# Attention steps put into a written-out cycle and pinned to program order on four engines

## Chip, core and metric

One core of a Trainium2 chip runs the whole kernel as one launch. The metric is the time of one launch in microseconds (us) of device time, lower is better; the time before is the median of three runs. All durations below are from one profiled execution of the kernel before.

## What is computed

One layer of a trunk: modulated RMS norm, one input projection, three token mixers (chunked gMLP, grouped-query attention, short gated convolution), an output projection, and a gated ConvFFN. The change lies in the attention, 1024 queries against 256 context keys and 1024 latent keys, 8 query heads in 2 key/value groups of 64 wide heads, in float32:

```python
def latent_attention(q, k_lat, v_lat, k_ctx, v_ctx):
    keys = jnp.concatenate([k_ctx, k_lat], axis=1)
    vals = jnp.concatenate([v_ctx, v_lat], axis=1)
    ...
    def block(qi):
        s = jnp.einsum('bqgrd,bkgd->bgrqk', qi, keys, preferred_element_type=jnp.float32) * ATT_SCALE
        p = jax.nn.softmax(s, axis=-1).astype(vals.dtype)
        return jnp.einsum('bgrqk,bkgd->bqgrd', p, vals)
    o = lax.map(block, qb)
```

## The kernel before

The attention is 16 units: 8 blocks of 128 queries times 2 key/value groups; a unit holds four heads. float32 products are made of a rounded part and a rest (fp32r), so each matmul below comes twice. Tiles and engines of one unit:

- `sc` (PSUM, one buffer): scores of two heads against the 256 context keys; four matmuls each on TensorE (PE).
- `sl` (PSUM, two buffers): scores of one head against the 1024 latent keys, four matmuls in two halves.
- VectorE (DVE) takes the row maxima of `sc` and `sl` and their common one (a 128x1 operation); ScalarE (ACT) writes the exponentials into `pp` (latent) and `pc` (context) with their row sums; DVE adds the two sums and takes the reciprocal (two 128x1 operations); GpSimd (POOL) multiplies `pc` and `pp` by it in place.
- `tr` (PSUM, two buffers): ten steps, one for each 128 keys, in which PE transposes the four heads' probabilities. ACT copies `tr` rounded into `ph`, DVE writes the rest `pw = tr - ph` (four buffers each), and PE adds value x `ph` and value x `pw` to `acc` (PSUM, one buffer).
- Tail: ACT copies the lower half of `acc` to `sh`, DVE adds the two halves into `af` (two operations), POOL splits `af` into two parts of `att`.

Helpers record every operation, so all rows of the profile show line 90. In the code, `scores` (line 281) makes the steps of the score part and `av` (line 973) those of the rest. Line 41 holds a cycle of tokens that is walked once for each unit (line 1015): `c` `a` `b` `p` `e` `z` are score steps of the newest unit, and `T`, `A`, `F` with a suffix are steps of a unit one or two cycles older. Three of these tokens stand for steps of several engines: `c` is matmul and maximum, `e` both exponentials, `z` sums, reciprocal and both POOL multiplications; `T` is transposes, copy and rest.

```python
PROG = "c0 T8+2 A5+2 a0 T9+2 b0 A6+2 A7+2 p0 e0 T0+1 A8+2 A9+2 F0+2 a1 T1+1 ..."
```

The tokens only say in what order the steps are recorded. From line 740 on nothing is pinned (`order("")`), so a scheduler in the compiler sets the order of each engine's queue from its own costs. Once built, each engine works through its queue strictly in that order; an instruction that waits holds up all behind it.

Into the cycle four kinds of side work are recorded at fixed points (`EV`, cycle number and fraction): `make_gB0` at 10.3 (PE makes two tiles `pgb` in the `tr` tag, ACT copies them to `gB`), `make_acm` at 11.3 (ACT rounds and DVE subtracts four `aT` and `cmT` slices of 128x512, two and two in one operation), and `w_out_part` four times at 11.5, 13, 15 and 15.1: it loads a piece `wo` of the output weights, POOL multiplies it by `gB` (two operations), ACT rounds it, DVE subtracts (`wos`). The first unit's scores are made earlier, between the matmuls `pcb` of the convolution gate (`X0`, line 40). Behind the attention the output projection (`po`) reads `acm`, `att` and `wos`.

Of the kernel before, what the change touches and what calls it, by code (L numbers as in the profile page):

```python
# [39 lines left out]
X0 = ("c0 a0 b0 p0 e0 z0 a1 b1 p1 e1 z1", "c1 a2 b2 p2 e2 z2 a3 b3 p3 e3 z3", "")  # L40
PROG = "c0 T8+2 A5+2 a0 T9+2 b0 A6+2 A7+2 p0 e0 T0+1 A8+2 A9+2 F0+2 a1 T1+1 b1 p1 e1 T2+1 c1 T3+1 z0 A0+1 a2 b2 p2 a3 A1+1 z1 e2 T4+1 T5+1 A2+1 A3+1 z2 b3 T6+1 p3 e3 A4+1 z3 T7+1"
AVO = sorted((i + 1000 * int(t[3:]), int(t[1])) for i, t in enumerate(PROG.split()) if t[0] == "A")
AVF, AVL = AVO[0][1], AVO[-1][1]
# [28 lines left out]
def trunk(  # L72
# [207 lines left out]

    def scores(tb, g):
        hf, i = tb // 4, tb % 4
        pl = []
# [30 lines left out]

        def soft(h):
            if h == 0:
# [5 lines left out]
                pl.append(box["pc"])  # L322
            if h % 2 == 0:
                box["pp"] = hp.tile([P, 2, NT], F32, name=f"pp{tb}{g}{h}", tag="h0", bufs=4)
            p_ = box["pp"][:, h % 2, :]
            pl.append(p_)
            S.activation(p_, box.pop(("sl", h)), AF.Exp, bias=v(2, h), accum_out=v(3, h))
            S.activation(box["pc"][:, h, :], box["sc"][:, h % 2, :], AF.Exp, bias=v(2, h),
                         accum_out=v(4, h))
# [7 lines left out]
        ops = {"c": ctx_mm, "a": lambda h: lat_mm(h, 0), "b": lambda h: lat_mm(h, 1),  # L337
               "p": top, "e": soft, "z": norm}

        def item(t):  # L340
            for o in t.split():
                ops[o[0]](int(o[1]))

        return item, pl
# [608 lines left out]
    def w_out_part(i):
        n2, q = i // 4, i % 4
        r = raw(f"wo{i}").rearrange("p (k n) -> p k n", k=2)
        dma(r, w_out[q * 256:(q + 1) * 256, n2 * 512:(n2 + 1) * 512]
            .rearrange("(k p) n -> p k n", p=P))
# [4 lines left out]
        wos.append(t_)

    with t_ctx:
# [7 lines left out]

        def av(tb, g, pl):
            hf, i = tb // 4, tb % 4
            box = {}
# [12 lines left out]
            def av_step(kb):
                if kb == AVF:
                    box["acc"] = pst.tile([P, 512], F32, name=f"acc{tb}{g}", tag="acc", bufs=1)  # L990
                acc = box["acc"]
# [2 lines left out]
                T.matmul(acc, vv, ph, start=kb == AVF, stop=False)
                T.matmul(acc, vv, pw, start=False, stop=kb == AVL)

            def fin(_):
                acc = box["acc"]
                sh = tp.tile([64, 512], F32, name=f"sh{tb}{g}", tag="sh", bufs=1)
                S.copy(sh, acc[64:128, :])  # L1000
                af = tp.tile([P, 2, P], F32, name=f"af{tb}{g}", tag="af", bufs=1)
                a4 = acc[0:64, :].rearrange("p (i e t) -> p i e t", i=2, e=2)
                s4 = sh.rearrange("p (i e t) -> p i e t", i=2, e=2)
# [4 lines left out]
                G.tensor_scalar(hi, af, 1.0, 1.0, ALU.mult, ALU.mult)
                G.tensor_tensor(lo, af, f(hi), ALU.subtract)

            return tr_step, av_step, fin

        xs, vs = {}, {0: av(0, 0, pl0)}
        prog = PROG.split()
        for n in range(len(prog), 20 * len(prog)):
            u_, at = n // len(prog), n % len(prog)
            if at == 0 and u_ < 16:
                xs[u_], pl = scores(u_ // 2, u_ % 2)
                vs[u_] = av(u_ // 2, u_ % 2, pl)
            t = prog[at]  # L1020
            if t[0] in "TAF":
                k, d = t[1:].split("+")
                if 0 <= u_ - int(d) < 16:
                    vs[u_ - int(d)]["TAF".index(t[0])](int(k))
            elif u_ < 16:
                xs[u_](t)
# [576 lines left out]
```

## Time and profile before

| | |
|---|---|
| time, median of 3 runs | 1302.74 us (1302.57 to 1303.81) |
| the profiled execution | 1302.53 us, of which the span from first to last instruction is 1300.7 us |
| busy share of the span | PE 95%, DVE 75%, ACT 47%, POOL 36% |
| attention, first score matmul to last `acc` matmul | 249.7 to 519.4 us |
| tail copies `sh<-acc`, one for each unit | first at 284.18 us, last at 519.38 us |

The attention takes about a fifth of the span. The copy `sh<-acc` comes once in each unit, so the distance of two of these copies is the period of the cycle. A row of the time line gives start, duration, engine, operation, output and input tiles (buffer numbers left out), and in brackets the engine's idle time before it and what ended it. Two instructions of one engine overlap a little at their ends, so the cost of one in a full queue is the distance from its start to the next start, not its duration.

### The profile page before, as it was taken

The numbers are of one execution on the slowest core, as the hardware profiler recorded it, in microseconds if no ns is written. First come the engines' busy times: TensorE is split into PE (matmuls) and PEld (weight loads), VectorE is DVE, ScalarE is ACT, GpSimd is POOL, SyncE is SP. The second block draws the span as 40 slices with busy tenths as digits, with TensorE's granted clock in tenths as the row PEclk, the third lists the DMA queues.
The fourth block names the chain that finished last, engine by engine and source line by source line (L and its number), as shares of the span: only waits on it lengthen the run. The fifth ranks groups of instructions, "written<-read, shape, count | busy, mean of one in ns | idle before, by whom it ended". The sixth has DMA issues, their size and how long they took to land.

```text
span 1300.7 us, 17813 instructions
## 1 busy us (share of the span) xinstructions
PE 1242.1 (95%) x6420; PEld 1028.0 (79%) x6420; DVE 978.5 (75%) x1700; ACT 614.2 (47%) x1116; POOL 463.0 (36%) x445
## 2 busy tenths in 40 slices
PE   6989999999998899999799999999999999999997
PEld 3879899877776677888588888888888888878885
DVE  4797777389989997686989899998678765225545
ACT  5753234277777777124554344344444534213331
POOL 1252243044446543542655544544453110030001
PEclk9999999999999999999899999999999999999999
DMA  9906001000000000963033433332230349023741
GB/s 289 280 19 193 28 31 50 17 1 2 1 2 1 1 1 19 326 195 142 0 98 98 130 97 103 124 98 90 89 98 33 130 173 363 15 95 132 259 178 65
DMA packets 109190, 132.15 MB, mean 102 GB/s; under 512 B 7632, under 2 KB 77998, under 8 KB 109102
## 3 DMA queue, kind: packets, MB, share of 16 engines
q1 hardware_dynamic: 109102, 131.01, 30.2%
q8 instruction: 51, 0.84, 0.3%
q14 instruction: 37, 0.30, 0.1%
HBM read 111.07 MB, written 19.92 MB: 101 GB/s over the span
## 4 chain that ended last, share of the span: by engine, by line
PE 83%; DVE 7%; ACT 4%; issue 2%; POOL 2%; DMA 1%; SPq 0%; POOLq 0%; DVEq 0%; ACTq 0%
PE pd L90 19%; PE pY L90 14%; PE pZ L90 9%; PE pX L90 9%; PE acc L90 5%; PE po L90 5%; PE tr L90 4%; PE pq L90 3%; PE sl L90 3%; PE pau L90 2%; PE pcc L90 2%; PE pcb L90 2%; PE pav L90 2%; PE pch L90 2%; PE sc L90 1%
## 5 line engine op out<-in xcount | busy, mean ns | idle before, releaser
L90 PE MATMUL pd<-wd,gt 128*128 128x512 f32 x912 | 209.2, 391 | 3.2 <-DVE wd L90 3.2
L90 PEld LDWEIGHTS pd<-wd,gt 128*128 128x128 f32 x912 | 172.1, 189 | 39.8 <-DVE wd L90 3.9
L90 PE MATMUL pY<-HT,wM 128*128 128x512 f32 x792 | 192.9, 392 | 6.7 <-DVE HT L90 3.9
L90 PEld LDWEIGHTS pY<-HT,wM 128*128 128x128 f32 x792 | 148.8, 189 | 39.4 <-DVE HT L90 4.4
L90 DVE TENSOR_TENSOR wM<-wu,wM 128x512 fp32r<-128x512 f32 x132 | 135.0, 1025 | 12.7 <-ACT wM L90 12.3
L90 ACT CAST wM<-wu 128x512 fp32r<-128x512 f32 x132 | 80.6, 620 | 111.3 <-PE pY L90 54.9
L90 PE MATMUL pX<-HB,wM 128*128 128x512 f32 x528 | 127.4, 389 | 0.0
L90 DVE TENSOR_TENSOR pw<-tr,ph 128x512 fp32r<-128x512 f32 x160 | 108.9, 684 | 14.2 <-ACT ph L90 13.6
L90 ACT CAST ph<-tr 128x512 fp32r<-128x512 f32 x160 | 92.1, 596 | 56.0 <-PE tr L90 55.3
L90 PEld LDWEIGHTS pX<-HB,wM 128*128 128x128 f32 x528 | 99.0, 188 | 20.5
L90 PE MATMUL sl<-K,Q 128*128 128x512 f32 x256 | 82.8, 408 | 8.1 <-ACT pp L90 8.1
L90 POOL TENSOR_TENSOR wu<-S,wu 128x512 f32<-128x512 f32 x22 | 29.4, 1335 | 169.9 <-DVE wM L90 169.7
L90 POOL TENSOR_SCALAR pc<-pc,sm 128x256 f32<-128x256 f32 x64 | 31.8, 497 | 148.5 <-DVE sm L90 102.7
L90 PE MATMUL tr<-ident,pp 128*128 128x128 f32 x512 | 80.1, 275 | 4.3 <-DVE pw L90 4.3
L90 PEld LDWEIGHTS tr<-ident,pp 128*128 128x128 f32 x512 | 61.7, 140 | 25.1 <-DVE pw L90 12.0
L90 DVE TENSOR_REDUCE sm<-sl 128x1 f32<-128x1024 f32 x64 | 77.5, 1213 | 0.4
L90 ACT CAST gt<-g 128x512 fp32r<-128x512 f32 x38 | 23.5, 619 | 108.3 <-DMA g<-gud 79.2
L90 ACT ACTIVATE pp<-sl,sm 128x1024 f32<-128x1024 f32 x64 | 72.2, 1128 | 4.8 <-DVE sm L90 4.7
L90 POOL TENSOR_SCALAR pp<-pp,sm 128x1024 f32<-128x1024 f32 x64 | 73.0, 1141 | 0.0
L90 DVE TENSOR_TENSOR wd<-wd,wd 128x1024 fp32r<-128x1024 f32 x44 | 55.7, 1266 | 18.0 <-ACT wd L90 15.7
L90 DVE TENSOR_TENSOR gt<-g,gt 128x512 fp32r<-128x512 f32 x38 | 26.1, 687 | 56.1 <-ACT gt L90 56.1
L90 PE MATMUL pZ<-HT,wM 128*128 128x512 f32 x264 | 66.1, 396 | 1.6 <-DVE HT L90 1.6
(341 smaller groups left out, 2798.1 us busy)
## 6 DMA issues: line engine op xcount, KB each, us to landing
wu<-in_ffn_up SPq DMA_DIRECT2D x88, 256.0 KB, 3.1
wd<-in_ffn_down SPq DMA_DIRECT2D x44, 512.0 KB, 7.8
w<-in_w_mod SPq DMA_DIRECT2D x24, 512.0 KB, 4.4
g<-gud SPq DMA_DIRECT2D x44, 256.0 KB, 4.7
wm<-in_w_mod SPq DMA_DIRECT2D x16, 512.0 KB, 6.7
wi<-in_w_in SPq DMA_DIRECT2D x16, 512.0 KB, 6.1
gud<-y SPq DMA_DIRECT2D x11, 512.0 KB
gud<-ya SPq DMA_DIRECT2D x11, 512.0 KB, 2.9
```

The lines of the kernel that those rows point to most:

```text
L90: i = fn(*a, **k)
```

## The change

`scores` and `av` no longer give compound tokens but one token for each step of one engine, and line 41's cycle is written anew over 83 tokens with suffix `+1` or `+2` for steps of the unit one or two cycles older. The letters, used from here on: on PE `C` context scores, `a` and `b` latent scores, `T` transposes, `A` the two products with the values; on DVE `x` and `p` maxima, `m` common maximum, `n` sum and reciprocal, `L` rest, `d` sum of the halves; on ACT `c` and `e` exponentials, `K` rounded copy, `f` tail copy; on POOL `y` and `z` multiplications, `g` output. `order("TVSG")` pins PE, DVE, ACT and POOL to the recorded order through the whole cycle. The `wo` loads are recorded one cycle before the other work on them (`WOL`), and the last two pieces move from 15 and 15.1 to 16.1 and 16.3. The accumulation now always goes from key block 0 to 9.

```diff
-WO0 = (11.5, 13, 15, 15.1)
-PROG = "c0 T8+2 A5+2 a0 T9+2 b0 A6+2 A7+2 p0 e0 T0+1 A8+2 A9+2 F0+2 ... z3 T7+1"
+WO0 = (11.5, 13, 16.1, 16.3)
+WOL = 1
+X0 = ("C0 x0 a0 b0 p0 m0 e0 c0 n0 y0 z0 a1 b1 ...", "C1 x1 a2 b2 ...", "")
+PROG = ("a0 L5+2 m3+1 n1+1 L6+2 z1+1 A4+2 b0 y1+1 T7+2 c3+1 K7+2 e3+1 p0 A5+2 C0 T8+2 A6+2 "
+        "K8+2 L7+2 T9+2 n2+1 x0 n3+1 m0 L8+2 K9+2 y2+1 a1 c0 y3+1 A7+2 b1 e0 L9+2 z3+1 z2+1 "
+        "A8+2 T0+1 K0+1 A9+2 f+2 T1+1 K1+1 p1 m1 a2 b2 L0+1 T2+1 d+2 A0+1 c1 L1+1 C1 T3+1 e1 "
+        "g+2 a3 K2+1 p2 K3+1 A1+1 L2+1 T4+1 K4+1 b3 A2+1 x1 L3+1 m2 T5+1 e2 n0 K5+1 L4+1 A3+1 "
+        "T6+1 z0 K6+1 y0 p3 c2")
...
-        def norm(h):
+        def recip(h):
             V.tensor_scalar(v(5, h), v(3, h), v(4, h), None, ALU.add)
             V.reciprocal(v(6, h), v(5, h))
-            for t_ in (box["pc"][:, h, :], pl[h + 1]):
-                G.tensor_scalar(t_, t_, v(6, h), 1.0, ALU.mult, ALU.mult)
+        def norm(h, at):
+            G.tensor_scalar(pl[at, h], pl[at, h], v(6, h), 1.0, ALU.mult, ALU.mult)
...
-        EV += [(w, lambda: w_out_part(len(wos))) for w in WO0]
+        EV += [(w - WOL, lambda i=i: w_out_part(i)) for i, w in enumerate(WO0)]
+        EV += [(w, lambda i=i: w_out_split(i)) for i, w in enumerate(WO0)]
...
+            def hi_step(kb):
+                ph = box["ph", kb] = tp.tile([P, 512], F32R, name=f"ph{tb}{g}{kb}", tag="ph",
+                                             bufs=PH)
+                S.copy(ph, box["tr", kb])
+            def lo_step(kb):
+                pw = box["pw", kb] = tp.tile([P, 512], F32R, name=f"pw{tb}{g}{kb}", tag="pw",
+                                             bufs=PH)
+                sub_lo(pw, box.pop(("tr", kb)), box["ph", kb])
...
+        order("TVSG")
+        for n in range(len(prog), (16 + lags) * len(prog)):
...
+            o, k, l = prog[at]
+            if 0 <= u_ - l < 16 and not (u_ == l and o in ops0):
+                us[u_ - l][o](k)
             for e, f_ in EV:
                 if n == int(e * len(prog)):
                     f_()
+        order("")
```

No instruction is added or removed on any engine, and the queue of SP, which issues all loads and stores, keeps its order. Three places follow; `sm` holds a unit's 128x1 values, and the numbers are those of buffers in the built program.

DVE in a plain cycle before: a stretch of eight rows in which `TENSOR_TENSOR pw` is a step `L`.

```order
L90 TENSOR_REDUCE sm_74<-sl_5821 128x1
L90 TENSOR_TENSOR pw_5796<-tr_5790,ph_5795 128x512
L90 TENSOR_REDUCE sm_74<-sc_5799 128x2
L90 TENSOR_TENSOR pw_5811<-tr_5805,ph_5810 128x512
L90 TENSOR_SCALAR sm_74<-sm_74 128x1 x2
L90 TENSOR_TENSOR pw_5846<-tr_5840,ph_5845 128x512
L90 RECIPROCAL sm_74<-sm_74 128x1
L90 TENSOR_REDUCE sm_74<-sl_5828 128x1
```

The same queue after the change, from `p0` to `p1`.

```order
L94 TENSOR_REDUCE sm_72<-sl_5304 128x1
L94 TENSOR_TENSOR pw_5348<-tr_5322,ph_5328 128x512
L94 TENSOR_SCALAR sm_75<-sm_75 128x1
L94 RECIPROCAL sm_75<-sm_75 128x1
L94 TENSOR_REDUCE sm_72<-sc_5334 128x2
L94 TENSOR_SCALAR sm_75<-sm_75 128x1
L94 RECIPROCAL sm_75<-sm_75 128x1
L94 TENSOR_SCALAR sm_72<-sm_72 128x1
L94 TENSOR_TENSOR pw_5361<-tr_5339,ph_5346 128x512
L94 TENSOR_TENSOR pw_5378<-tr_5350,ph_5363 128x512
L94 TENSOR_REDUCE sm_72<-sl_5366 128x1
```

What moved: sum and reciprocal now stand directly behind each other, and two steps `L` stand together behind `m0`.

DVE around the side work of cycle 11 before.

```order
L90 TENSOR_TENSOR acm_5191<-aT,acm_5190 128x1024
L90 TENSOR_TENSOR pw_5051<-tr_5045,ph_5050 128x512
L90 TENSOR_SCALAR sm_74<-sm_74 128x1
L90 TENSOR_TENSOR pw_5086<-tr_5080,ph_5085 128x512
L90 TENSOR_REDUCE sm_74<-sl_5068 128x1
L90 TENSOR_TENSOR acm_5191<-cmT,acm_5190 128x1024
L90 TENSOR_TENSOR pw_5095<-tr_5089,ph_5094 128x512
```

And after the change:

```order
L94 TENSOR_SCALAR sm_75<-sm_75 128x1
L94 TENSOR_TENSOR acm_5164<-aT,acm_5163 128x1024
L94 TENSOR_TENSOR acm_5164<-cmT,acm_5163 128x1024
L94 TENSOR_TENSOR pw_5169<-tr_5141,ph_5148 128x512
L94 TENSOR_TENSOR pw_5186<-tr_5152,ph_5171 128x512
L94 TENSOR_TENSOR wos_5205<-wo_5010,wos_5205 128x1024
L94 TENSOR_REDUCE sm_75<-sl_5174 128x1
```

What moved: the two `acm` stand together between `m0` and `L8`, and the first `wos` stands between `L9` and `p1`; before, a whole unit of steps lay between them.

POOL behind the reciprocals of the same cycle, after the change (before, the four pieces `wo` followed each other in one run of eight operations).

```order
L94 TENSOR_SCALAR pc_4984<-pc_4984,sm_74 128x256 x3
L94 TENSOR_SCALAR pp_5087<-pp_5087,sm_74 128x1024 x2
L94 TENSOR_TENSOR wo_5010<-wo_5010,gB_3301 128x512 x2
L94 TENSOR_SCALAR att_3307<-af_5229 128x2x128
L94 TENSOR_TENSOR att_3308<-af_5229,att_3307 128x2x128
```

What moved: the multiplication of one `wo` piece now stands behind all of a unit's `y` and `z` and ahead of `g`. In cycle 13 the second piece stands on POOL behind `y0`, on ACT ahead of `c3`, and on DVE ahead of `L5`.

## Rows read from the trace of the kernel before

**Rows 1.** Stretches, columns: us, busy of PE, PEld, DVE, ACT, POOL, PEclk, DMA, GB/s.

```profile
336.00:353.00 17.00, 15.88 (x94) 12.73 (x93) 15.50 (x35) 13.66 (x31) 7.57 (x11) 1.00 0.00 1
```

**Rows 2.** Time line of ACT: tail copies of units 0, 7 and 13.

```profile
284.18 0.58 ACT L90 COPY sh<-acc 64x512 f32<-64x512 f32 x1
...
393.18 0.58 ACT L90 COPY sh<-acc 64x512 f32<-64x512 f32 x1
...
493.15 0.58 ACT L90 COPY sh<-acc 64x512 f32<-64x512 f32 x1
```

**Rows 3.** Time line of DVE inside one period.

```profile
346.33 0.21 DVE L90 TENSOR_SCALAR sm<-sm 128x1 f32<-128x1 f32 x1 [0.28 <-ACT pc L90]
346.57 0.17 DVE L90 RECIPROCAL sm<-sm 128x1 f32<-128x1 f32 x1
347.00 0.85 DVE L90 TENSOR_TENSOR af<-acc,sh 64x256 f32<-64x256 f32 x2 [0.26 <-ACT sh L90]
347.88 0.69 DVE L90 TENSOR_TENSOR pw<-tr,ph 128x512 fp32r<-128x512 f32 x1
348.49 1.22 DVE L90 TENSOR_REDUCE sm<-sl 128x1 f32<-128x1024 f32 x1
349.62 0.68 DVE L90 TENSOR_TENSOR pw<-tr,ph 128x512 fp32r<-128x512 f32 x1
350.22 0.68 DVE L90 TENSOR_REDUCE sm<-sc 128x2 f32<-128x512 f32 x1
...
353.74 0.33 DVE L90 TENSOR_SCALAR sm<-sm 128x1 f32<-128x1 f32 x2
353.99 0.68 DVE L90 TENSOR_TENSOR pw<-tr,ph 128x512 fp32r<-128x512 f32 x1
354.59 0.15 DVE L90 RECIPROCAL sm<-sm 128x1 f32<-128x1 f32 x1
354.66 0.67 DVE L90 TENSOR_TENSOR pw<-tr,ph 128x512 fp32r<-128x512 f32 x1
```

**Rows 4.** Time line of ACT and POOL in the same period.

```profile
347.41 1.12 ACT L90 ACTIVATE pp<-sl,sm 128x1024 f32<-128x1024 f32 x1
...
348.51 0.47 ACT L90 ACTIVATE pc<-sc,sm 128x256 f32<-128x256 f32 x1
...
348.96 1.09 ACT L90 CAST ph<-tr 128x512 fp32r<-128x512 f32 x2
...
347.39 1.12 POOL L90 TENSOR_SCALAR pp<-pp,sm 128x1024 f32<-128x1024 f32 x1
```

**Rows 5.** Time line of PE in the same period.

```profile
359.04 0.60 PE L90 MATMUL tr<-ident,pc 128*128 128x128 f32 x4
359.39 0.48 PE L90 MATMUL acc<-pw,V 128*128 128x512 f32 x1
359.71 0.40 PE L90 MATMUL acc<-ph,V 128*128 128x512 f32 x1
359.94 0.39 PE L90 MATMUL acc<-pw,V 128*128 128x512 f32 x1
```

**Rows 6.** Time lines of POOL and DVE: side work in cycles 10 to 14.

```profile
412.50 1.29 POOL L90 TENSOR_TENSOR wo<-wo,gB 128x512 f32<-128x512 f32 x1
...
414.43 2.39 DVE L90 TENSOR_TENSOR acm<-aT,acm 128x1024 fp32r<-128x1024 f32 x1
...
489.83 1.22 DVE L90 TENSOR_TENSOR wos<-wo,wos 128x1024 fp32r<-128x1024 f32 x1
```

**Rows 7.** Stretches (columns of Rows 1) and time line of PE: clock and pauses.

```profile
10.00:20.00 10.00, 8.19 (x25) 2.83 (x24) 5.27 (x19) 4.76 (x8) 1.43 (x2) 0.84 1.12 307
404.00:421.00 17.00, 14.21 (x85) 11.25 (x84) 15.00 (x25) 14.70 (x28) 13.26 (x13) 1.00 0.01 1
...
417.47 0.66 PE L90 MATMUL tr<-ident,pp 128*128 128x128 f32 x4 [1.97 <-DVE pw L90]
```

**Rows 8.** Stretch (columns of Rows 1): the end of the attention.

```profile
506.00:523.00 17.00, 16.94 (x93) 13.07 (x91) 11.55 (x19) 9.44 (x16) 4.64 (x6) 1.00 0.16 63
```

More of the change, by code (lines that the diff above doesn't have):

```diff
@@ L38 @@
 AC0 = 11.3
-WO0 = (11.5, 13, 15, 15.1)
[L40 to L43, printed above, removed]
+WO0 = (11.5, 13, 16.1, 16.3)
+WOL = 1
+X0 = ("C0 x0 a0 b0 p0 m0 e0 c0 n0 y0 z0 a1 b1 p1 m1 e1 c1 n1 y1 z1", "C1 x1 a2 b2 p2 m2 e2 c2 n2 y2 z2 a3 b3 p3 m3 e3 c3 n3 y3 z3", "")
+PROG = ("a0 L5+2 m3+1 n1+1 L6+2 z1+1 A4+2 b0 y1+1 T7+2 c3+1 K7+2 e3+1 p0 A5+2 C0 T8+2 A6+2 "
[4 rows of a table added]
+AVF, AVL = 0, 9
 CX = 1
@@ L282, in scores @@
         hf, i = tb // 4, tb % 4
-        pl = []
+        pl = {}
         st = sm[(2 * tb + g) % 4]
@@ L308, in v, with lat_max, both_max, lat_exp @@
             return st[:, 4 * n + h:4 * n + h + 1]
-        def top(h):
-            V.tensor_reduce(v(0, h), box["sl"], axis=AX.X, op=ALU.max, negate=True)
+        def lat_max(h):
+            V.tensor_reduce(v(0, h), box["sl", h], axis=AX.X, op=ALU.max, negate=True)
+        def both_max(h):
             V.tensor_scalar(v(2, h), v(0, h), v(1, h), None, ALU.min)
-            box["sl", h] = box["sl"]
-        def soft(h):
-            if h == 0:
+        def lat_exp(h):
+            if h % 2 == 0:
+                box["pp"] = hp.tile([P, 2, NT], F32, name=f"pp{tb}{g}{h}", tag="h0", bufs=4)
+            pl[1, h] = box["pp"][:, h % 2, :]
+            S.activation(pl[1, h], box.pop(("sl", h)), AF.Exp, bias=v(2, h), accum_out=v(3, h))
+        def ctx_exp(h):
+            if "pc" not in box:
                 if (tb, g) == (0, 0):
@@ L321, in soft @@
                                                bufs=2)
[L322 to L328, printed above, removed]
+            pl[0, h] = box["pc"][:, h, :]
+            S.activation(pl[0, h], box["sc", h // 2][:, h % 2, :], AF.Exp, bias=v(2, h),
                          accum_out=v(4, h))
-        def norm(h):
+        def recip(h):
             V.tensor_scalar(v(5, h), v(3, h), v(4, h), None, ALU.add)
             V.reciprocal(v(6, h), v(5, h))
-            for t_ in (box["pc"][:, h, :], pl[h + 1]):
-                G.tensor_scalar(t_, t_, v(6, h), 1.0, ALU.mult, ALU.mult)
[L337 to L344, printed above, removed]
+        def norm(h, at):
+            G.tensor_scalar(pl[at, h], pl[at, h], v(6, h), 1.0, ALU.mult, ALU.mult)
+        return {"C": ctx_mm, "x": ctx_max, "a": lambda h: lat_mm(h, 0),
+                "b": lambda h: lat_mm(h, 1), "p": lat_max, "m": both_max, "e": lat_exp,
+                "c": ctx_exp, "n": recip, "y": lambda h: norm(h, 0), "z": lambda h: norm(h, 1)}, pl
     h_ctx = ExitStack()
@@ L926, in trunk @@
                 psb["b1"] = (pst, "tr", 2)
-                item, pl0 = scores(0, 0)
+                ops0, pl0 = scores(0, 0)
             if i >= 1:
-                item(X0[i - 1])
+                for t in X0[i - 1].split():
+                    ops0[t[0]](int(t[1]))
     gbp = ctx.enter_context(tc.tile_pool(name="gbp", bufs=1, side="right", reuse_waits="tile"))
@@ L951, in trunk, with w_out_split @@
     wos = []
+    wol = {}
     def w_out_part(i):
         n2, q = i // 4, i % 4
-        r = raw(f"wo{i}").rearrange("p (k n) -> p k n", k=2)
+        r = wol[i] = raw(f"wo{i}").rearrange("p (k n) -> p k n", k=2)
         dma(r, w_out[q * 256:(q + 1) * 256, n2 * 512:(n2 + 1) * 512]
             .rearrange("(k p) n -> p k n", p=P))
+    def w_out_split(i):
+        n2, r = i // 4, wol.pop(i)
         for kk in range(2):
@@ L991, in av_step, with lower, both @@
                 acc = box["acc"]
-                ph, pw = box.pop(kb)
                 vv = VC[:, kb, g, :] if kb < 2 else Vt[:, kb - 2, g, :]
[L994 to L1003, printed above, removed]
+                T.matmul(acc, vv, box.pop(("ph", kb)), start=kb == AVF, stop=False)
+                T.matmul(acc, vv, box.pop(("pw", kb)), start=False, stop=kb == AVL)
+            def lower(_):
+                box["sh"] = tp.tile([64, 512], F32, name=f"sh{tb}{g}", tag="sh", bufs=1)
+                S.copy(box["sh"], box["acc"][64:128, :])
+            def both(_):
+                af = box["af"] = tp.tile([P, 2, P], F32, name=f"af{tb}{g}", tag="af", bufs=1)
+                a4 = box["acc"][0:64, :].rearrange("p (i e t) -> p i e t", i=2, e=2)
+                s4 = box["sh"].rearrange("p (i e t) -> p i e t", i=2, e=2)
                 for e in range(2):
@@ L1006, in fin, with att_out @@
                                     ALU.add)
+            def att_out(_):
                 hi, lo = [att[hf][l][:, 2 * g:2 * g + 2, i * P:(i + 1) * P] for l in range(2)]
[L1008 to L1015, printed above, removed]
+                G.tensor_scalar(hi, box["af"], 1.0, 1.0, ALU.mult, ALU.mult)
+                G.tensor_tensor(lo, box["af"], f(hi), ALU.subtract)
+            return {"T": tr_step, "K": hi_step, "L": lo_step, "A": av_step, "f": lower,
+                    "d": both, "g": att_out}
+        us = {0: {**ops0, **av(0, 0, pl0)}}
+        prog = [(t[0], int(t[1:2].strip("+") or 0),
+                 int(t.partition("+")[2] or 0)) for t in PROG.split()]
+        lags = max(l for _, _, l in prog) + 1
+        order("TVSG")
+        for n in range(len(prog), (16 + lags) * len(prog)):
             u_, at = n // len(prog), n % len(prog)
             if at == 0 and u_ < 16:
[L1018 to L1026, printed above, removed]
+                sc_, pl = scores(u_ // 2, u_ % 2)
+                us[u_] = {**sc_, **av(u_ // 2, u_ % 2, pl)}
+            o, k, l = prog[at]
+            if 0 <= u_ - l < 16 and not (u_ == l and o in ops0):
+                us[u_ - l][o](k)
             for e, f_ in EV:
@@ L1310, in trunk @@
             w_out_part(len(wos))
+            w_out_split(len(wos))
     fcr = w4("fcr", [P, 1024], F32).rearrange("p (h n) -> p h n", h=8)[0:66]
```

23 lines of the change are left out of this document (11 added, 12 removed).

## The prediction

> **What bounds the kernel now.** I read the busy table by stretch first. In a plain stretch of 17 us in the middle of the attention VectorE (DVE) is busy for 15.50 us, TensorE (PE) for 15.88, ScalarE (ACT) for 13.66 and GpSimd (POOL) for 7.57; the granted clock is 1.00 and the DMA engines stand still [rows 1]. No transfer and no clock bounds this stage; it is the queues of PE and DVE, and how they wait for each other. Then the tail copies: the first and the eighth are 393.18 - 284.18 = 109.00 us apart, so a plain cycle takes 109.00 / 7 = 15.57 us. From the first to the fourteenth there are 208.97 us, 13 cycles; at 15.57 they would take 202.4, so the side work of cycles 10 to 13 costs 6.6 in the old order [rows 2].
>
> The time line of DVE then gives what each step costs in a full queue, as the distance of two starts [rows 3]: a rest `L` 0.60 (353.99 to 354.59), a latent maximum `p` 1.13, the two additions `d` 0.88, sum with reciprocal `n` 0.24 + 0.07 = 0.31, a common maximum `m` 0.13 (two in 0.25). A context maximum `x` shows a duration like an `L` in its group and is taken at 0.60. One cycle has 10 `L`, 4 `p`, 2 `x`, one `d`, 4 `m`, 4 `n`: 6.0 + 4.52 + 1.2 + 0.88 + 0.52 + 1.24 = 14.36; one `m` stands directly behind its own `p` now, 0.08 for its wait by the 0.20 that a 128x1 operation takes less the 0.12 it costs in the queue; together **14.4 us**. The period is 15.57, so 1.17 us of each cycle are waits of DVE. They are small and of several kinds: 0.28 for `pc` from ACT, 0.26 for `sh` from ACT [rows 3]. That is what a better order can win, and no more, for no instruction is removed and DVE cannot go below 14.4.
>
> PE has little more room. Ten times transposes 0.35, product with `pw` 0.32, product with `ph` 0.23 [rows 5] are 9.0; 16 latent score matmuls at 0.23 are 3.7; eight for the context keys, with half the columns, lie between 0.115 and 0.23 each, 0.9 to 1.8. The sum is 13.6 to 14.5, so PE too is nearly full at 14.4, and I keep that as a reason for the first rival.
>
> **The plain cycle, walked.** I lay the new DVE queue out with these costs, `L5` at 0: `m3` 0.60, `n1` 0.73, `L6` 1.04, `p0` 1.64, `L7` 2.77, `n2` 3.37, `x0` 3.68, `n3` 4.27, `m0` 4.58, `L8` 4.70, `L9` 5.30, `p1` 5.90, `m1` 7.11, `L0` 7.24, `d` 7.84, `L1` 8.72, `p2` 9.32, `L2` 10.45, `x1` 11.05, `L3` 11.64, `m2` 12.24, `n0` 12.36, `L4` 12.67, `p3` 13.27, end 14.40. Then I ask for each when its input is there, with 1.10 for an exponential over 1024 keys, 0.45 for one over 256, 0.55 for a rounded copy [rows 4] and 0.60 for four transposes to land [rows 5]. Four chains are short. `L8` reads its buffer out at 5.38; `A8` and the transposes `T0` follow, `T0` lands at about 6.5, the copy `K0` ends at 7.16, and `L0` is due at 7.24: margin 0.08. `A9` ends near 7.0, the tail copy `f` (0.58, [rows 2]) near 7.65, `d` is due at 7.84: about 0.1 to 0.2. On ACT `K1`, `c1`, `e1`, `K2` follow one another to 10.3, and `L2` is due at 10.45: 0.15. `L2` frees the buffer of `T4`, `K4` ends at 12.5, `L4` is due at 12.67: 0.15. All others have 0.3 or more. So the order holds on paper with small margins. Their slip is not in the trace: nothing if the margins hold, 0.8 a cycle as the bound of the first rival; I take 0.1, since the four margins are 0.08 to 0.2 and the durations repeat to about 0.02 [rows 3]: 13 x 0.1 = **1.3**.
>
> **The side work** is where an order that nothing may leave costs most, because a waiting instruction now holds up its engine's queue.
> - Cycle 10, `make_gB0`: both `pgb` tiles come at one place behind `L8` and, counted through the two `tr` buffers, each waits for the other's copy. `pgb` lands 0.6 after 5.4, copy to 6.6, second `pgb` 7.3, copy 7.9, then `K9` to 8.5, and `L9` starts at 8.5 where 5.3 was due: **+3.2**.
> - Cycle 11, `acm` and the first `wos`: on POOL `y3`, `z3`, `z2` (1.12 each `z`, [rows 4]) end near 7.6, two `wo` multiplications of 1.29 [rows 6] end at 10.2, a rounding on ACT, taken at the 1.12 of an equally wide operation [rows 4], at 11.3, the subtraction of 1.22 [rows 6] at 12.5. Behind it stands `p1`, due at 5.90: +6.6. The two `acm` stand in the same queue ahead of it; of them one took 2.39 while POOL multiplied `wo`, against 1.22 for a `wos` of the same size [rows 6]. If they hold POOL up by as much, up to +9.0. I take the middle, **+7.8**.
> - Cycle 13, the second piece: `z0` and `y0` end near 0.2 of the next cycle, `wo` 2.8, rounding 3.9, subtraction 5.1, and `L5` was due at 0: **+5.0**.
>
> Sum 16.0, against 6.6 before: this takes 9.4 back. The bounds are DVE's own time for these four operations, 4 x 1.22 = 4.9, and 17.2 (with the 9.0). What hides the loads of `wo`: they are recorded a cycle ahead and DMA is idle there [rows 1]. The Trainium skill says under "SBUF — State Buffer", section "Who interferes with whom", that VectorE with two inputs from SBUF and GpSimd share a port pair, and whichever holds it shuts the other out; the doubled `acm` agrees, and by that rule alone the cycle would cost the 9.0 and the total would be 1.2 later.
>
> The last two pieces come in cycle 16, behind the last unit's scores, where PE is full with output projection work (16.94 of 17 us in the old order, [rows 8]). They cost nothing while PE has that work; without the cover each would cost DVE's 1.22. Taken at 0, between -1.5 and +1.5. The start-up cycle, which now records the first two units' scores pinned, is taken at 0, between -1 and +1 by about the 1.17 of waits that one cycle holds.
>
> **The sum.** 13 x 14.4 = 187.2; + 1.3 + 16.0 = 204.5 against 208.97: -4.5. The profiled execution took 1302.53, so 1298.0; it lies 0.2 below the median, which gives **1298.2 us**. The bounds of the terms give this case its own range, 1294 to 1302.7 (no gain).
>
> **Rivals.**
> - *The margins fail.* Break-even is a period of (208.97 - 16.0) / 13 = 14.84, so 0.44 of waits in a cycle use the whole gain up. The place is the loop `L8`, `A8`, `T0`, `K0`, `L0` and the one from `L2` over `T4`, `K4` to `L4`: a copy that starts 0.4 late on ACT stops `L0`, which stops `d`, `L1` and the transposes behind them, and no other instruction may pass. For it: a semaphore step between engines is only in part in my distances, PE's sum reaches 14.5, and in the old order DVE waits twice by over 0.25 in a space of 0.7 us [rows 3]. Against it: each engine by itself fits in 14.5. At 15.2, half way between break-even and the old period, it is 13 x 15.2 + 16.0 = 213.6, +4.6: **1307.3 us**, slower.
> - *TensorE's clock falls.* In cycle 11 PE stands still for some 5.8 us, in cycle 13 for some 4.8, longer than the 1.97 us at which the clock stayed 1.00 in the old order [rows 7]. Early in the kernel, where PE had run with gaps, a stretch of 10 us was granted 0.84 of full clock [rows 7]: 1.6 us lost. Twice that is 3.2: **1301.4 us**, no change. The Trainium skill, "TensorE: Matmul & The Clock Gate", section "Why this matters for your kernels", says that idle gaps between bursts of matmuls take the engine back to half its clock; at 2.4 GHz here the old trace shows no such gap in the attention, so nothing yet bears it out.
> - *The side work hides.* If POOL is earlier than I walk it, only DVE's own 4.9 remain: 187.2 + 1.3 + 4.9 = 193.4, -15.6: **1287.1 us**. Against it: `wo` stands behind all `y` and `z` on POOL by the order shown, and `p1` behind `wos`.
>
> That the order isn't kept by the built program is excluded: the queues shown are those that run.
>
> **How the numbers follow.** The forecast gets 0.50, failing margins 0.22, the clock 0.16, hidden side work 0.12. About 0.2% (2.6 us) is what a measurement of this kernel can tell from no change. Faster by more: 0.36 of the forecast's 0.50, 0.06 of the clock, 0.12 of the last, 0.54. Within: 0.13, 0.08 and 0.02 of the margins, 0.23. Slower: 0.01, 0.20 and 0.02, 0.23. The range 1290 to 1307 leaves out about half of the failing margins above and most of the last rival below, 0.2 in all.
>
> **What would show it.** In the new profile the tail copies in plain cycles should be 14.4 to 14.6 apart and DVE nearly without idle time there; 15 or more, with waits in front of `L0`, `d` or `L4`, is the first rival. The distances should grow by 3.2 in cycle 10, 7.8 in cycle 11 (DVE waiting for `wo` in front of `wos`) and 5.0 in cycle 13; under 2 each is the last rival. The granted clock behind these pauses tells the second. I am wrong in the sum's frame if the distance from the last tail copies to the end of the attention moves by over 1.5 us.

## The result and the profile after

The change made the kernel 0.6% slower. Median 1310.91 us (1309.77 to 1311.31, six runs) against 1302.65 (1302.04 to 1303.81, six runs): ratio 1.0061, interval 1.0048 to 1.0074. Forecast was 1298.2, faster. The profiled execution has a span of 1309.0 us against 1300.7.

The time line of ACT, the tail copies of the changed kernel (the answers to [rows 2]):

```profile
286.12 0.58 ACT L94 COPY sh<-acc 64x512 f32<-64x512 f32 x1
...
387.12 0.58 ACT L94 COPY sh<-acc 64x512 f32<-64x512 f32 x1
405.99 0.58 ACT L94 COPY sh<-acc 64x512 f32<-64x512 f32 x1
423.08 0.58 ACT L94 COPY sh<-acc 64x512 f32<-64x512 f32 x1 [0.21 <-PE acc L94]
445.26 0.58 ACT L94 COPY sh<-acc 64x512 f32<-64x512 f32 x1
466.13 0.58 ACT L94 COPY sh<-acc 64x512 f32<-64x512 f32 x1
...
495.07 0.58 ACT L94 COPY sh<-acc 64x512 f32<-64x512 f32 x1
517.51 0.58 ACT L94 COPY sh<-acc 64x512 f32<-64x512 f32 x1
528.62 0.58 ACT L94 COPY sh<-acc 64x512 f32<-64x512 f32 x1 [1.32 <-PE acc L94]
```

Read the distances. From the first to the eighth copy 101.00 us, 14.43 a cycle against 15.57 before: the plain cycle does what was walked. Then 18.87 (gB), 17.09 (acm), 22.18 (first wos), 20.87 (second wos): 4.44 + 2.66 + 7.75 + 6.44 = 21.29 us of side work against 6.6 before. From the first to the fourteenth copy it comes to 208.95, before 208.97: what the shorter period won in 13 cycles, 14.8 us, is spent by the side work, which costs 14.7 more. Behind the fourteenth, the last two units take 33.55 us, before (508.20 and 519.38 were its last two copies) 26.23: 7.3 more, and that is the loss, with 1.9 at the start and 0.9 won back behind the attention.

Stretches of the changed kernel (columns as in [rows 1]): the same plain stretch, then single pieces of the cycle with the first wos and of the one with the second, then the end (answers to [rows 1, 8]).

```profile
336.00:353.00 17.00, 16.76 (x101) 13.70 (x100) 16.75 (x37) 14.97 (x35) 8.86 (x13) 1.00 0.00 1
...
420.00:421.00 1.00, 0.00 (x0) 0.00 (x0) 1.00 (x3) 0.98 (x2) 1.00 (x2) 1.00 0.00 0
421.00:422.00 1.00, 0.96 (x6) 0.89 (x7) 0.58 (x1) 0.00 (x0) 1.00 (x2) 0.81 0.00 0
422.00:425.00 3.00, 3.00 (x11) 2.38 (x10) 0.00 (x0) 1.17 (x2) 3.00 (x3) 0.50 0.00 0
425.00:428.00 3.00, 0.40 (x2) 0.00 (x0) 1.58 (x2) 1.63 (x2) 0.31 (x1) 0.99 0.00 0
...
429.00:435.00 6.00, 5.32 (x19) 4.53 (x20) 5.25 (x11) 2.83 (x6) 1.14 (x2) 0.50 0.00 0
...
455.00:463.00 8.00, 4.83 (x21) 4.34 (x22) 6.26 (x15) 3.89 (x7) 2.96 (x6) 0.57 0.00 0
...
506.00:523.00 17.00, 15.29 (x73) 11.62 (x72) 9.70 (x16) 9.04 (x16) 10.40 (x10) 0.90 0.00 1
```

In the plain stretch DVE is busy for 16.75 of 17 us where it was 15.50. In the cycle of the first wos PE works at half its clock (0.50, the level of 1.2 GHz) from 422 to 425, stands still, while the granted clock reads 0.99, and works at half again from 429 to 435. In the old order the clock is 1.00 in the whole attention.

The time lines of the four engines there, in the order DVE (with the second wos), ACT, POOL, PE; a bracket gives the idle time and what ended it:

```profile
418.02 1.23 DVE L94 TENSOR_TENSOR acm<-aT,acm 128x1024 fp32r<-128x1024 f32 x1
419.16 1.22 DVE L94 TENSOR_TENSOR acm<-cmT,acm 128x1024 fp32r<-128x1024 f32 x1
426.42 1.22 DVE L94 TENSOR_TENSOR wos<-wo,wos 128x1024 fp32r<-128x1024 f32 x1 [4.84 <-ACT wos L94]
434.13 0.69 DVE L94 TENSOR_TENSOR pw<-tr,ph 128x512 fp32r<-128x512 f32 x1 [0.70 <-ACT ph L94]
...
456.29 1.23 DVE L94 TENSOR_TENSOR wos<-wo,wos 128x1024 fp32r<-128x1024 f32 x1 [3.64 <-ACT wos L94]
...
425.34 1.04 ACT L94 CAST wos<-wo 128x1024 fp32r<-128x1024 f32 x1 [1.68 <-POOL wo L94]
...
417.17 0.48 POOL L94 TENSOR_SCALAR pc<-pc,sm 128x256 f32<-128x256 f32 x1 [1.05 <-ACT ph L94]
418.08 2.57 POOL L94 TENSOR_SCALAR pc<-pc,sm 128x256 f32<-128x256 f32 x1 [0.43 <-DVE sm L94]
422.80 2.51 POOL L94 TENSOR_TENSOR wo<-wo,gB 128x512 f32<-128x512 f32 x2
...
421.04 0.50 PE L94 MATMUL acc<-pw,V 128*128 128x512 f32 x1 [2.02 <-DVE pw L94]
429.68 1.12 PE L94 MATMUL tr<-ident,pp 128*128 128x128 f32 x4 [4.28 <-DVE pw L94]
```

The chain can be read backwards: DVE waits 4.84 us for ACT's rounding, that for POOL's two multiplications, and these begin only at 422.80, behind a unit's `y` and `z`. PE stands for 4.28 us because the rest `L0` it needs is queued behind the waiting wos. In cycle 13 DVE waits 3.64 us in the same way. One of the `y` takes 2.57 us on POOL while DVE subtracts the two acm; the one ahead of it took 0.48. The Trainium skill, "SBUF — State Buffer", section "Who interferes with whom", says that the one of VectorE and GpSimd that holds their shared port pair shuts the other out; the 2.57 against 0.48 agrees.

### The profile page after: what moved, and what is told of

Its sections match the earlier page's. It is cut to its first block, busy times and chain, and to the rows that moved or that the text cites. A ratio compares the mean times of both kernels' runs of the same rounds, so it can differ in the third digit from the quotient of the medians.

```text
span 1309.0 us, 17795 instructions
## 1 busy us (share of the span) xinstructions
PE 1248.8 (95%) x6420; PEld 1038.2 (79%) x6420; DVE 977.1 (75%) x1700; ACT 620.5 (47%) x1116; POOL 463.3 (35%) x445
## 4 chain that ended last, share of the span: by engine, by line
PE 72%; DVE 19%; POOL 2%; ACT 2%; issue 2%; DMA 2%; SPq 0%; POOLq 0%; DVEq 0%; ACTq 0%
PE pd L94 18%; PE pY L94 14%; PE pZ L94 9%; PE pX L94 9%; DVE sm L94 8%; DVE pw L94 6%; PE po L94 5%; PE pq L94 3%; PE pau L94 2%; PE pcc L94 2%; PE pcb L94 2%; PE pav L94 2%; PE pch L94 2%; PE pm L94 1%; PE acc L94 1%
## 5 line engine op out<-in xcount | busy, mean ns | idle before, releaser
L94 DVE TENSOR_TENSOR wM<-wu,wM 128x512 fp32r<-128x512 f32 x132 | 135.0, 1025 | 12.7 <-ACT wM L94 12.4
L94 DVE TENSOR_TENSOR pw<-tr,ph 128x512 fp32r<-128x512 f32 x160 | 107.9, 682 | 13.5 <-ACT ph L94 12.8
L94 DVE TENSOR_TENSOR wd<-wd,wd 128x1024 fp32r<-128x1024 f32 x44 | 55.7, 1266 | 16.5 <-ACT wd L94 14.4
L94 PE MATMUL pZ<-HB,wM 128*128 128x512 f32 x264 | 64.3, 392 | 0.0
```

The lines of the kernel that those rows point to most:

```text
L94: i = fn(*a, **k)
```

## Experiments

Each run stands beside runs of the kernel before on the same chip; the last column is the ratio to these, and a gain "by the ratios" is the difference of two of these, multiplied by 1302.65 us. Theory A: the waits in pinned queues cost. Theory B: the half clock behind PE's pauses costs beside them. Theory C: the last two pieces stand at the wrong place.

| kernel | median us | ratio, 95% interval |
|---|---|---|
| the change | 1310.91 | 1.0061 [1.0048, 1.0074] |
| e1_halves | 1301.68 | 0.9988 [0.9979, 0.9997] |
| e2_nomul | 1301.83 | 0.9985 [0.9976, 0.9994] |
| e3_old_places | 1313.21 | 1.0075 [1.0061, 1.0089] |
| e4_fill | 1306.22 | 1.0025 [1.0016, 1.0035] |
| e5_early | 1292.48 | 0.9911 [0.9896, 0.9926] |
| e6_unpinned | 1305.84 | 1.0015 [1.0006, 1.0025] |
| e7_pin_to_10 | 1297.10 | 0.9953 [0.9938, 0.9968] |
| e8_old_order | 1507.23 | 1.1564 [1.1547, 1.1581] |
| e9_ahead | 1288.62 | 0.9884 [0.9869, 0.9899] |
| e10_only_early | 1306.22 | 1.0013 [1.0005, 1.0022] |
| e11_only_wo | 1295.65 | 0.9940 [0.9928, 0.9952] |

**e1_halves**

```diff
-WOL = 1
+WOM = (10.69, 12.69, 14.69, 15.69)
+WOD = (9.5, 11, 13, 14)
...
+    def w_out_mul(i):
+        n2, r = i // 4, wol[i]
+        for kk in range(2):
+            G.tensor_tensor(r[:, kk, :], r[:, kk, :], gB[0][:, n2 * 512:(n2 + 1) * 512], ALU.mult)
+
     def w_out_split(i):
-        n2, r = i // 4, wol.pop(i)
-        for kk in range(2):
-            G.tensor_tensor(r[:, kk, :], r[:, kk, :], gB[0][:, n2 * 512:(n2 + 1) * 512], ALU.mult)
+        r = wol.pop(i)
...
+        EV += [(w, lambda i=i: w_out_part(i)) for i, w in enumerate(WOD)]
+        EV += [(w, lambda i=i: w_out_mul(i)) for i, w in enumerate(WOM)]
```

> The POOL multiplications of each wo piece are recorded one step behind g of cycles 10, 12, 14 and 15, half a cycle to a cycle ahead of its rounding and subtraction, which keep their places; the loads one cycle earlier. Theory A (the chain POOL, ACT, DVE inside one place of pinned queues is what costs: 4.84, 3.64 and 4.74 us of waiting in front of wos): the waits are gone, each piece costs DVE's 1.2 to 1.5; tail copy distances behind units 9 and 10 fall from 22.18 and 20.87 to about 15.8 each, the last two units from 33.55 to 26 to 28, time about 1293 us (1291 to 1296). Theory C (the last two pieces stand at the wrong place, whatever feeds them): the last two units stay at 32 to 34 us, time 1298 to 1301. A theory in which the side work's own instructions cost: no gain over 3 us.

Measured 1301.7: by the ratios 9.5 us won of the 18 expected. The distances of the two wos cycles are 19.69 and 17.39 (were 22.18 and 20.87), the last two units 27.22 (were 33.55). So theory C falls: with the same places and POOL ahead, the end is back within 1 us of the old 26.23. But A was only half served. The time line of DVE in this kernel:

```profile
423.64 1.23 DVE L95 TENSOR_TENSOR wos<-wo,wos 128x1024 fp32r<-128x1024 f32 x1 [3.06 <-ACT wos L95]
...
450.86 1.23 DVE L95 TENSOR_TENSOR wos<-wo,wos 128x1024 fp32r<-128x1024 f32 x1 [1.74 <-ACT wos L95]
```

DVE still waits 3.06 and 1.74 us, now for the rounding alone. The first rounding stands in ACT's queue behind the tail copy, and that behind `A9` and `L9`; the second stands behind ACT's own copies and exponentials: the piece waits for the very cycle it is put in. And of 13.4 us by which the last tail copy comes earlier (528.62 to 515.24) the span shows 10.5. The traces hold the rest: 41 output projection matmuls (`po`) run before the last tail copy in the change and 29 here, and 12 at 0.23 us [rows 5] are 2.8 us of work that now comes later.

**e2_nomul**

```diff
-        for kk in range(2):
+        for kk in range(2 if i > 3 else 0):
             G.tensor_tensor(r[:, kk, :], r[:, kk, :], gB[0][:, n2 * 512:(n2 + 1) * 512], ALU.mult)
```

> The POOL multiplications of the four wo pieces in the attention are left out (the output projection uses these pieces without the gate); rounding and subtraction stay where they are. Theory A: as with the multiplications moved, 1291 to 1295 us, no wait of DVE for wos over 1 us. Theory that the work of ACT and DVE at these places costs, not the wait: 1307 us or more.

Measured 1301.8, the same as e1_halves within the intervals, with distances of 19.35, 17.40 and 27.30. It missed the 1291 to 1295 in the same way: DVE still waits 3.39 and 1.74 us, since POOL was one link and the place of rounding and subtraction another. Leaving POOL's work out is worth no more than recording it earlier, so no cost of the work itself shows.

**e3_old_places**

```diff
-WO0 = (11.5, 13, 16.1, 16.3)
+WO0 = (11.5, 13, 15, 15.1)
```

> The last two wo pieces go back to cycle fractions 15.0 and 15.1, all else as changed. Theory A: the waits only move, cycle 15 grows by 7 to 10 us and the end shrinks by about as much or less: 1309 to 1314 us. Theory C (the new places in the last cycle are the mistake): the last two units and the output projection win 5 to 7 us, 1303 to 1306 us.

Measured 1313.2: cycle 15 grows to 25.83 and the last two distances are 13.63 and 11.16, 24.79 where the change has 33.55. DVE waits 3.63 and 4.71 us for the two pieces in cycle 15. The wait goes where the piece goes.

**e4_fill**

```diff
+FILLS = {(11, "b", 1): 4, (11, "b", 2): 10, (13, "b", 0): 8}
...
                 us[u_ - l][o](k)
+                if (u_, o, k) in FILLS:
+                    for _ in range(FILLS[u_, o, k]):
+                        us[u_][o](k)
```

> PE repeats score matmuls it has just made, with the same result, in front of its pauses: 8 behind b1 and 20 behind b2 in cycle 11, 16 behind b0 in cycle 13. Theory B (the half clock behind the pauses costs 3 to 5 us beyond the waits): granted clock 1.00 from 420 to 465 us although PE does 10 us more work, distances of 22.18 and 20.87 us shrink by 1.5 to 3 each, time 1306 to 1308 us. Theory A alone (only the waits cost): clock back at 1.00, time as after the change, 1310 to 1312 us.

Measured 1306.2, 4.7 us less than the change, with 44 matmuls more. The distances fall from 17.09 to 16.69, from 22.18 to 20.59 and from 20.87 to 19.33. Time line of DVE and PE, and stretches:

```profile
425.50 1.23 DVE L95 TENSOR_TENSOR wos<-wo,wos 128x1024 fp32r<-128x1024 f32 x1 [4.88 <-ACT wos L95]
453.35 1.23 DVE L95 TENSOR_TENSOR wos<-wo,wos 128x1024 fp32r<-128x1024 f32 x1 [3.66 <-ACT wos L95]
...
421.67 5.74 PE L95 MATMUL sl<-K,Q 128*128 128x512 f32 x24
428.76 0.66 PE L95 MATMUL tr<-ident,pp 128*128 128x128 f32 x4 [1.35 <-DVE pw L95]
```

```profile
425.00:430.00 5.00, 3.46 (x17) 2.48 (x16) 4.42 (x7) 2.91 (x7) 0.40 (x1) 1.00 0.00 0
430.00:435.00 5.00, 5.00 (x34) 4.18 (x33) 4.96 (x10) 3.12 (x7) 2.00 (x3) 1.00 0.02 5
```

PE's pause is 1.35 us instead of 4.28, the clock stays at 1.00, and four transposes behind it take 0.66 us, not 1.12. DVE waits as long as in the change, 4.88 us against 4.84 here and 3.66 in cycle 13; only the waits for copies behind it, 0.70 and more, are gone. So this is the clock's own price: theory B holds beside A, at 0.40 + 1.59 + 1.54 = 3.5 us in the distances. The time falls by 4.7, but 0.9 of that lies ahead of the first tail copy (285.19 against 286.12), where no matmul was added. At the end, where none was added either, the clock is 0.50 for about 3 us in both kernels, and the last two units take 33.55 us in both. The Trainium skill, "TensorE: Matmul & The Clock Gate", section "Why this matters for your kernels", says that idle gaps between bursts of matmuls take the engine back to half its clock; the 0.50 behind the pause of 4.28 us agrees. That not every gap does so here is told in the last section.

**e10_only_early** and **e11_only_wo** take the side work apart.

```diff
-GB0 = 10.3
-AC0 = 11.3
+GB0 = 1.05
+AC0 = 1.02
```

> The changed kernel with gB and acm alone moved to cycle 1; the wo pieces as changed. Theory A with B: cycle 10 back to 14.4 (from 18.87), the one behind it to 14.4 (from 17.09), the pause of 2.02 us in front of the first wos gone and with it the first stretch of half clock; the wo cycles stay near 20 to 22, the end near 33.5, cycle 1 costs 2 to 3: time 1304 to 1307 us.

```diff
-WO0 = (11.5, 13, 16.1, 16.3)
-WOL = 1
+WO0 = (11.84, 12.84, 16.1, 16.3)
+WOC = (11.74, 12.74, 16.08, 16.28)
+WOM = (10.69, 11.69, 14.69, 15.69)
+WOD = (9.5, 11, 13, 14)
...
+        EV += [(w, lambda i=i: w_out_mul(i)) for i, w in enumerate(WOM)]
+        EV += [(w, lambda i=i: w_out_hi(i)) for i, w in enumerate(WOC)]
         EV += [(w, lambda i=i: w_out_split(i)) for i, w in enumerate(WO0)]
```

> The changed kernel with the wo pieces alone split in three; gB and acm at their places in cycles 10 and 11. Theory A: distances 18.9 and 17.1 stay, those of 22.18 and 20.87 fall to 15.6 to 16.5, the last two units to 27 to 28; 1295 to 1299 us. If gB and acm were the larger part of the loss: 1303 us or more.

Both times came as expected: gB and acm moved alone give 1306.2, their cycles 14.41 and 14.43, the wos cycles still 22.21 and 20.41; the wo pieces split in three alone (`w_out_hi` is ACT's rounding, `w_out_split` keeps DVE's subtraction; the loads and POOL's work come earlier too) give 1295.7, with 15.76 and 15.52 and an end of 27.23. By the ratios (1.0061 less 1.0013 and less 0.9940) gB and acm are worth 6.3 us and the wo pieces 15.8. In e10_only_early the pause of 2.02 us and the half clock right behind it are gone, as expected, and yet the wos cycle is as long as before: DVE waits 5.13 us in front of the first wos there, PE stands 6.10, and the clock is 0.50 from 422 to 428.

One expectation for e11_only_wo missed: gB's cycle takes 20.32 us, not 18.9. The pauses in front of the two `pgb` are those of the change, 1.28 and 0.68 us, but here the clock fell behind them. Time line of PE and stretches in e11_only_wo:

```profile
401.49 2.08 PE L96 MATMUL pgb<-ident,mod 128*128 128x128 f32 x8 [0.68 <-ACT gB L96]
...
422.31 0.50 PE L96 MATMUL acc<-pw,V 128*128 128x512 f32 x1 [2.06 <-DVE pw L96]
```

```profile
401.00:405.00 4.00, 3.51 (x12) 3.20 (x13) 0.29 (x1) 1.83 (x5) 0.72 (x1) 0.57 0.00 0
...
420.00:430.00 10.00, 7.75 (x48) 6.11 (x47) 9.92 (x15) 8.08 (x17) 7.75 (x7) 1.00 0.01 2
```

The second `pgb` takes 2.08 us where the change has 1.16 (shown further down). e2_nomul has the same cycle at 20.29, again with the clock at 0.50.

**e5_early** is both together, with the first piece a cycle earlier.

> Side work taken out of each other's way: gB and acm go into cycle 1, where DVE has no rests of an older unit; each wo piece is split in three, POOL in the cycle before, the rounding behind K3 where ACT had 0.78 us idle, the subtraction behind L3; the last two pieces as in e1_halves. Theory A with B (waits in pinned queues, and the half clock that follows pauses of PE): the plain 14.4 us in all cycles but two, these at 15.6 to 16; granted clock 1.00 throughout; 6 to 9 us below e1_halves, 1293 to 1296 us. Theory D (PE's fixed work and the start take back what the middle wins): 1299 to 1302 us.

Measured 1292.5, a little better than expected, and by the ratios 19.5 us less than the change where the two parts add up to 22.0. Time lines of DVE and PE around a subtraction:

```profile
408.35 0.68 DVE L96 TENSOR_TENSOR pw<-tr,ph 128x512 fp32r<-128x512 f32 x1
408.95 1.22 DVE L96 TENSOR_TENSOR wos<-wo,wos 128x1024 fp32r<-128x1024 f32 x1
410.08 0.33 DVE L96 TENSOR_SCALAR sm<-sm 128x1 f32<-128x1 f32 x2
...
411.25 0.66 PE L96 MATMUL tr<-ident,pp 128*128 128x128 f32 x4 [0.87 <-DVE pw L96]
```

No wait ahead of it: the piece costs the 1.13 us from its start to the next, and the cycle 15.57 instead of 14.43. The other eleven distances among the first fourteen copies are 14.42 to 14.44. What stays is a first tail copy at 288.40, some 3 us later than in e1_halves (285.13), and a clock that is not 1.00 throughout: it is 0.66 from 273 to 278.

**e9_ahead** is e5_early with gB and acm ahead of the loop; the diff shows that part alone.

```diff
-        EV = [(GB0, make_gB0),
-              (AC0, lambda: make_acm(0, [mx(f"acm0{l}", [P, 4, 512]) for l in range(2)]))]
...
+        make_gB0()
+        make_acm(0, [mx(f"acm0{l}", [P, 4, 512]) for l in range(2)])
+        EV = []
```

> As e5_early, but gB and acm are recorded ahead of the pinned loop, unpinned, where DVE and ACT stand nearly idle beside the matmuls of the convolution gate. If the 3 us that e5_early lost before its first tail copy (288.40 against 285.2 us) are these operations in cycle 1: first tail copy at 285 to 286, time 1289 to 1291 us. If they are not: 1292 to 1294.

Measured 1288.6, the best of all, 15.4 us below the kernel before on the same chip. The time came just under what was expected, the first tail copy did not: 287.66. Stretches of this kernel:

```profile
240.00:290.00 50.00, 47.95 (x249) 39.25 (x249) 32.02 (x62) 27.32 (x58) 13.26 (x18) 1.00 0.00 1
...
380.00:470.00 90.00, 86.77 (x514) 70.17 (x513) 88.69 (x184) 78.87 (x167) 53.45 (x68) 1.00 0.00 1
```

For the change the second stretch reads 76.34 us of PE, 73.37 of DVE, at a clock of 0.91. In e5_early the clock from 240 to 290 is 0.97, here 1.00, but that is little of the gain over e5_early. Of the 3.3 us between the spans (1290.5 and 1287.2), 0.7 lie before the first tail copy (288.40 and 287.66), 0.1 between it and the last, and 2.4 behind the attention: there PE pauses for 1.99 us in the output projection instead of 2.88, and the clock is 0.57 in 4 us (570 to 574) instead of in 8 (570 to 578). No run takes these by themselves. The first tail copy is late in part because PE makes both `pgb` ahead of it, 2.10 us from 266.57; how much of the 2.5 us against e1_halves that is stays open.

**What pinning does: e6, e7, e8**

```diff
-        order("TVSG")
+        order("")
```

> The new cycle and events as changed, but with nothing pinned, so the compiler's scheduler sets the queues again. If pinning is what makes the plain period: 15.4 to 15.6 us as before, side work as before, 1300 to 1305 us. If the recorded order alone does it: 14.4 to 14.8 and 1292 to 1297 us.

```diff
+            if n == 10 * len(prog):
+                order("")
```

> Pinned through cycle 9 only; from cycle 10 on the scheduler may place the side work and all else. Theory A: seven or eight plain cycles at 14.4 (8 us won), the rest about as before the change (15.5 us and some 6.6 of side work), 1294 to 1298 us. If the loss behind cycle 10 comes from the new cycle itself or the new places and not from pinning: 1305 us or more.

```diff
-PROG = ("a0 L5+2 m3+1 n1+1 L6+2 z1+1 A4+2 b0 ..."
+PROG = 'C0 x0 T8+2 K8+2 L8+2 A5+2 a0 T9+2 K9+2 L9+2 b0 ...'
```

> The old cycle, each compound token written out into its single steps in the old sequence, pinned on all four engines; events as changed. If the order of single steps is what makes 14.4: each L stands directly behind its own K and T, the period is 17 to 20 us and the time 1330 to 1370 us. If pinning any sound order is enough: 14.4 to 15, 1308 to 1315 us.

Unpinned, the new cycle gives plain distances of 15.13 to 15.18 behind the first, between the two that were expected, and 1305.8 us, above both. Pinned through cycle 9 only, it gives 14.4 up to there, then 17.11, 22.63, 16.36, 15.88 and an end of 26.27, and 1297.1 us, as expected: the loss behind cycle 10 belongs to pinning from there on, where the side work stands. The old sequence, pinned, takes 27.4 to 29.5 us a cycle and 1507 us, far beyond what was expected. Its DVE:

```profile
335.16 0.69 DVE L90 TENSOR_TENSOR pw<-tr,ph 128x512 fp32r<-128x512 f32 x1 [2.26 <-ACT ph L90]
...
358.77 0.69 DVE L90 TENSOR_TENSOR pw<-tr,ph 128x512 fp32r<-128x512 f32 x1 [2.29 <-ACT ph L90]
```

Most rests wait for their own copies, up to 2.29 us, and nothing may pass. The granted clock of PE is 0.70 from 336 to 353. So neither the new order nor pinning alone makes 14.43: it takes both. What was pinned here is the old sequence as it is recorded; the queues that the scheduler had made from it were pinned in no run.

## Why the prediction was wrong

**The plain cycle was right.** 14.4 us plus 0.1 of slip were forecast, 14.43 measured; waits of DVE are down to 17.00 - 16.75 = 0.25 in 17 us. The margins of 0.08 to 0.2 held, so the first rival, which held 0.20 of the 0.23 given to a slower kernel, was the wrong reason to fear a loss.

**The step that failed most** is "They cost nothing while PE has that work", on the last two pieces, taken at 0 between -1.5 and +1.5. The last two units took 7.3 us more, far over the 1.5 that the prediction had named as the sign of a wrong frame. The cover was the output projection, but that reads these very pieces, and the rests of the last unit are queued behind them. Time lines of DVE, POOL and PE at the end of the changed kernel:

```profile
508.81 1.22 DVE L94 TENSOR_TENSOR wos<-wo,wos 128x1024 fp32r<-128x1024 f32 x1 [4.74 <-ACT wos L94]
...
505.18 6.00 POOL L94 TENSOR_TENSOR wo<-wo,gB 128x512 f32<-128x512 f32 x4
...
508.83 0.49 PE L94 MATMUL po<-wos,att 128*128 128x512 f32 x1 [1.71 <-ACT wos L94]
```

DVE waits 4.74 us for the third piece, as it does for the first. PE has 15.29 of 17 us of work where [rows 8] had 16.94, at a clock of 0.90. I had walked this chain for cycles 11 and 13 and then excused the third place from it by a row of the old order, in which no such chain ran: there POOL's eight multiplications end at 423.90, and DVE subtracts at 425.25, 430.28, 489.83 and 492.16 without waiting. e1_halves takes 6.3 of these 7.3 us out of the distances without moving the pieces, and in e3_old_places the end without them is 24.79, so 8.8 us of the 33.55 are theirs.

**The second step** is the clock, held apart as a rival of 0.16 although its mechanism comes on top of the sum: it is not an alternative to the waits that I forecast but follows them. It fell in cycles 11 and 13 and at the end, and PE works at 0.50 behind each of the eight pauses of 4.20 to 6.10 us that it makes in the attention of the change, e3_old_places and e10_only_early. Cycle 13 shows the split: DVE's wait and subtraction were forecast at 5.0 and are 4.87 (3.64 and 1.23), yet the cycle grew by 6.44; with PE kept at work in e4_fill it grew by 19.33 - 14.43 = 4.90, the walked price. The side work as a whole was 21.3 against 16.0, and e4_fill puts 3.5 of these 5.3 us on the clock. The rival's own price for it, 3.2, was about right.

**Smaller terms.** gB was +3.2 and cost 4.44, because a `pgb` tile was priced like four transposes, 0.6, and takes 1.16. The time lines of PE and DVE in cycle 10:

```profile
399.83 1.16 PE L94 MATMUL pgb<-ident,mod 128*128 128x128 f32 x8 [1.28 <-DVE pw L94]
401.66 1.16 PE L94 MATMUL pgb<-ident,mod 128*128 128x128 f32 x8 [0.68 <-ACT gB L94]
...
403.96 0.69 DVE L94 TENSOR_TENSOR pw<-tr,ph 128x512 fp32r<-128x512 f32 x1 [4.19 <-ACT ph L94]
```

Cycle 11 was +7.8 and cost 2.66 + 7.75 = 10.4, of which 2.66 are the two acm standing between `m0` and `L8`. With PE kept at work in e4_fill it cost 2.26 + 6.16 = 8.4, between the 7.8 taken and the bound of 9.0, and the rest is the clock. The hold-up came the other way round from the row that I had used: the two acm took 1.23 and 1.22, not 2.39, and it was POOL that waited.

The start was 0 +- 1 and cost 1.9. Of this, 1.6 lie ahead of the first score matmul (251.25, before 249.66), where the change puts nothing, and the six other runs that are alike up to there begin it between 249.45 and 251.31. From that matmul to the first tail copy it is 34.87 against 34.52: 0.35 is the change's.

The 0.9 won back behind the attention is a balance. Before the last tail copy 41 `po` matmuls have run, in the old order 19; 22 at 0.23 us are 5.1 us of work done earlier. But then PE stands still in the middle of the output projection, waiting for a tile `mac` from DVE, and its clock falls; the old order has no such pause there. Time line of PE and a stretch of the changed kernel, then a stretch of the kernel before:

```profile
590.27 1.05 PE L94 MATMUL pm<-ones,mac 128*128 128x2 f32 x8 [2.61 <-DVE mac L94]
```

```profile
592.00:596.00 4.00, 4.00 (x13) 3.09 (x12) 2.54 (x11) 1.30 (x3) 0.55 (x1) 0.57 1.08 399
```

```profile
575.00:600.00 25.00, 24.91 (x122) 20.60 (x121) 16.55 (x39) 7.40 (x13) 8.63 (x12) 1.00 0.39 149
```

The pause is 2.61 us and the clock takes 4.00 x 0.43 = 1.7, which leaves 0.8. The same pause, 1.99 to 3.19 us, stands in e1_halves, e5_early, e9_ahead and e11_only_wo, so even the best kernel loses there.

The sum of it: 5.3 for side work, 7.3 for the end, 1.9 for the start, less 0.8 of slip not used and 0.9 won back later, is 12.8; the miss is 12.7.

**The third rival**, hidden side work, was rightly not what this order does, and its price was right for the two operations that a run shows: in e5_early a wo piece costs 15.57 - 14.43 = 1.14 us, near the 1.22 it was given. The two acm it moves out of these cycles altogether.

## What to carry to other kernels

When queues are pinned, work outside the cycle has to be cut into single steps just as the cycle is: each engine's part recorded where its input is long there, or the first waiting link stops all engines. Price such a chain wherever it occurs, also where another engine seems to have cover; ask whether the cover needs the same data. And where a forecast holds a long pause of TensorE, put the lower clock behind it into the sum, not among the rivals.

## What was not expected of the hardware

Matmuls added in front of a pause made the kernel faster: 44 more, 4.7 us less, of which 3.5 lie in the cycles that they were added to. The length of a pause alone did not tell whether the clock would fall: after a pause of 2.02 us in the change the next full microseconds were granted 0.50, after 1.97 in the old order 1.00 [rows 7], and after a pause of 2.06 at the same place in e11_only_wo the stretch from 420 to 430 us was granted 1.00 too. Behind pauses of 2.60 in cycle 13 of e1_halves and e2_nomul it stayed at 1.00, and the two short pauses at `pgb`, 1.28 and 0.68, left it at 1.00 in the change and were followed by 0.50 in e11_only_wo. What else decides is open here.
